# GpSimd's third block sum behind a lo part, and the short convolution's weight sums made by adding transfers

## The chip, the cores and the metric

One core of one Trainium2 chip runs the whole kernel. The metric is the time on the device in microseconds (us), the median over several runs. The core has TensorE (PE, matrix products), VectorE (DVE), ScalarE (ACT), GpSimd (POOL) and SyncE (SP), which run their own instruction lists in order and wait for each other by semaphores. Transfers between the chip's memory (DRAM) and the on-chip memory are issued from the queues of SP, ACT and POOL.

## The reference

One layer of a streaming encoder over 1024 positions and 1024 channels, all in float32:

```python
h = rms_norm(x, norm_mix_g[l]) * (1.0 + sc1) + sh1
proj = jnp.einsum('bsd,de->bse', h, w_in[l])
b_s, c_s, v_s, v_c, gl_c, gate_br = jnp.split(proj, SPLITS[:-1], axis=-1)
y_a = b_s * causal_dwconv(c_s * v_s, conv_short_w[l])
y_a = jnp.einsum('bsc,cd->bsd', y_a, w_short_out[l])
u = v_c * jax.nn.sigmoid(gl_c)
u = causal_dwconv(u, conv_conf_w[l]) + conv_conf_b[l]
u = jax.nn.silu(layer_norm(u, conf_ln_g[l], conf_ln_b[l]))
y_b = jnp.einsum('bsc,cd->bsd', u, w_conf_out[l])
g_a, g_b = jnp.split(jax.nn.sigmoid(gate_br), 2, axis=-1)
mix = jnp.einsum('bsd,de->bse', g_a * y_a + g_b * y_b, w_o[l])
x = x + g1 * mix
...
x = x + g2 * jnp.einsum('bsf,fd->bsd', jax.nn.silu(a) * bgate, w_ffn_out[l])
```

The change touches two of these products: `w_in` (the "input projection") and `w_short_out` (the "short convolution's projection", whose result is multiplied by the gate `g_a`).

## The kernel before

**Seven products instead of eight.** A weight is cut into "duals". A dual is two blocks of output rows by two halves of the inner dimension: four matrices of 128 x 1024 numbers, called 11, 12, 21 and 22. Its contribution is computed with seven products in the order 1, 2, 6, 5, 7, 3, 4 (`PRODUCTS`), in the manner of Strassen and Winograd. Products 1, 2 and 4 take the weights 11, 12 and 22 as they are. The others take sums: s1 = 21 + 22 (product 5), s2 = 11 + s1 (product 6), s3 = 21 + 11 (product 7), and 12 + s2 (product 3). These four block sums for each dual are the sums of the title.

**Hi and lo parts.** TensorE multiplies in a format with fewer bits, so every operand is split. ScalarE casts the weight to the hi part `wh` (line 234). VectorE or GpSimd subtracts: the lo part `wl` is the weight minus `wh` (line 235). Every product is 24 matmuls of 128 x 128 by 128 x 512: two output blocks, four inner blocks, and three combinations of hi and lo (lines 397, 398 and 400). Line 400 is the one that reads `wl`.

**Units.** The weight of one product, made ready, is a "unit": it loads what is missing into a `raw` buffer (line 218, on SP's queue), adds what has to be added, and calls `split_w`. `plan` lists the units, and `next_w` keeps two of them ready ahead of the product that runs. There are five raw buffers in this part of the kernel, and three each of `wh` and `wl`, so a unit's cast waits until the product three before it has left TensorE.

**The input projection** has 13 duals. `apart_units` makes the units of the first three, which the text calls the first, second and third input dual (d = 0, 1, 2). For the first, VectorE does sums and lo parts. For the second and third, GpSimd does the sums (line 312) and most lo parts: s1, s3 and s2 in product 6's unit, and 12 + s2 in product 3's. The third dual's products 1 and 2 run early, so that the products follow each other as: second dual 6, 5, 7, 3, 4, third dual 6, 5, ...

**The short convolution's projection** has two duals (0 and 1). Their 14 products run as 1, 1, 2, 2 (both duals), then 6, 5, 7, 3, 4 of dual 0 and the same of dual 1 (`ya_order`). `apart_units` makes these units too, with VectorE for all eight sums. Between the products VectorE also works on the other branch: it takes the mean from the convolution's result (`cv`, line 1015), adds up its squares (`sq`, line 1021), and splits the products' right sides (`q6l`, `q5l`, ..., line 913). `ya_evac` takes each product out of its accumulator and multiplies it by a gate tile `ga`, which is loaded from DRAM on GpSimd's queue (line 1088), 16 loads of 128 x 512.

**What sets the order.** The program is written once; a scheduler places the instructions of each engine and the transfers of each queue in a fixed list. `tc.issue_after(x)` tells it that an instruction has to stand behind x.

Of the kernel before, what the change touches and what calls it, by code (L numbers as in the profile page):

```python
# [38 lines left out]
ALU = mybir.AluOpType  # L39
# [76 lines left out]
PRODUCTS = "1265734"  # L116
# [15 lines left out]
def block_kernel(ctx: ExitStack, tc: tile.TileContext, x0, xT, c, vecs, ada, w_first, w_plain, w_duals,  # L132
                 w_short, w_conf, w_o, w_fi, w_fo0, w_fo1, outT):
    nc = tc.nc
# [30 lines left out]
    def ps2_tile(name):  # L165
        return ps2p.tile([P, H], F32, tag="ps2", name=name)
# [4 lines left out]
    def s_tile(name, dt=F32):  # L171
        return hl_tile(name, dt)

    def g_tile(name):
        return gsp.tile([P, H], F32, tag="gs", name=name)

    def f32(t):
        return t.bitcast(F32)

    halves = (slice(0, H), slice(H, T))  # L180
# [28 lines left out]
    def raw_tile(n=1024, home=None):  # L209

        if home is None:
            raws.append(raws.pop(0))
        return (home or raws[-1]).tile([P, 1024], F32, tag="raw", name="raw")[:, :n]

    def load(src, n=1024, home=None):
        raw = raw_tile(n, home)
        with tc.issue_after(x1_load[0]) if x1_load else ExitStack():
            load.ins = nc.sync.dma_start(raw, src).ins
        return raw
# [8 lines left out]
    def split_w(raw, n, after=(), lo_engine=nc.vector):  # L228
        wh = whp.tile([P, 1024], F32R, tag="wh", name="wh")[:, :n]
        wl = wlp.tile([P, 1024], F32R, tag="wl", name="wl")[:, :n]  # L230
        with ExitStack() as order:
            for ins in after:
                order.enter_context(tc.issue_after(ins))
            hi = nc.scalar.copy(wh, raw)  # L234
            lo = lo_engine.tensor_tensor(wl, raw, f32(wh), ALU.subtract)  # L235
        split_w.hi, split_w.lo = hi.ins, lo.ins
        if n == T and lo_engine is nc.gpsimd:
            pool_los.append((hi.ins, lo.ins))
        return wh, wl
# [66 lines left out]
    def apart_units(mats, eng, on_eng=PRODUCTS, after=None):  # L306


        a = {}

        def add(out, x, y):
            unit.eng.tensor_tensor(out, x, y, ALU.add)  # L312
            return out

        def get(b):
            return load(mats[("11", "12", "21", "22").index(b)])

        def unit(m):
            unit.eng = eng if m in on_eng else nc.gpsimd
            if m in "12":  # L320
                raw = get("1" + m)
            elif m == "6":
                for b in ("21", "22", "11"):
                    a[b] = get(b)
                with tc.issue_after(after()) if after else ExitStack():
                    a["s1"] = add(a["22"], a["21"], a["22"])
                    if "6" in on_eng:
                        raw = a["s2"] = add(raw_tile(), a["11"], a["s1"])
                    else:
                        a["s3"] = add(a["21"], a["21"], a["11"])  # L330
                        raw = a["s2"] = add(a["11"], a["11"], a["s1"])
            elif m == "7":
                raw = a["s3"] if "s3" in a else add(a["21"], a["21"], a["11"])
            elif m == "3":
                raw = get("12")
                add(raw, raw, a["s2"])
            else:
                raw = a["s1"] if m == "5" else get("22")
            return split_w(raw, 1024, (), unit.eng)

        return {m: (lambda m=m: unit(m)) for m in PRODUCTS}

    plan = [None] * KC
    plan += [(w_plain[0], 1024)]
    n_duals = len(PAIRS) // 2
    win_units = [apart_units([w_duals[d, m] for m in range(4)], nc.vector, PRODUCTS if d == 0 else "125" if d == 1 else "12",
                             (lambda: t_split.ins) if d == 1 else None) for d in range(BEGUN + 1)]
    win_units += [dual_units([w_duals[d, m] for m in range(4)], 1024, eng=nc.gpsimd) for d in range(BEGUN + 1, n_duals)]
    win_order = [(BEGUN, m) for m in "12"] + [(d, m) for d in range(BEGUN + 1) for m in PRODUCTS[2:]]
    win_order += [(d, m) for d in range(BEGUN + 1, n_duals) for m in PRODUCTS]  # L350
    plan += [win_units[d][m] for d, m in win_order]
    ya_order = [(d, m) for m in "12" for d in range(2)] + [(d, m) for d in range(2) for m in PRODUCTS[2:]]
    ya_units = [apart_units([w_short[d, m] for m in range(4)], nc.vector) for d in range(2)]
    plan += [ya_units[d][m] for d, m in ya_order]
    plan += [(w[k], 1024) for w in (w_conf, w_o) for ks in (range(KC), SECOND[KEPT:]) for k in ks]
    ready = []
# [212 lines left out]
    gate_dram = {(b, j): dram.tile([P, T], F32, name=f"gate_{b}{j}") for b in "ab" for j in range(KC)}  # L569
# [173 lines left out]
    def plus(out, ps, b):  # L743
        plus.ins = nc.vector.tensor_tensor(out, ps, b, ALU.add).ins
# [150 lines left out]
    b = {}  # L895
# [185 lines left out]
    def ya_evac(d, banks):  # L1081

        st = {}

        def out(i, row, h, op, ps):
            j = 4 * d + 2 * i + row
            ga = g_tile("ga")
            nc.gpsimd.dma_start(ga, gate_dram["a", j][:, halves[h]])
            ma[j, h] = s_tile(f"ma{j}{h}")
            op(ma[j, h], ps, ga)  # L1090
            ma["ins"] = plus.ins

        def evac(i, m, ps):
            if m == "1":
                if d == 1:
                    banks["y", i] = ps2_tile("y")
                nc.scalar.copy(banks["y", i], ps)
            elif m in "65":
                st[m, i] = s_tile("vz")
                nc.scalar.copy(st[m, i], ps)  # L1100
            elif m == "2":
                out(i, 0, 0, times, ps)
            elif m == "7":
                z = ps2_tile("z")
                plus(z, ps, st["5", i])
                out(i, 1, 1, minus_times, z)
            elif m == "3":
                plus(ps, ps, st["6", i])
                out(i, 0, 1, times, ps)
            else:  # L1110
                out(i, 1, 0, minus_times, ps)
        return evac
# [577 lines left out]
```

## Time and profile before

| what | value |
|---|---|
| median of 3 runs | 1460.13 us (1459.64, 1460.13, 1461.17) |
| the profiled execution, its time | 1462.66 us |
| its span, first to last instruction | 1460.9 us |
| TensorE's granted clock | 0.999 |
| busy: TensorE, VectorE, ScalarE, GpSimd | 1448.1, 1188.5, 627.2, 516.3 us |
| the input projection's stage, roughly | 90 to 562 us |
| the short convolution's projection | 562.2 to 643.0 us |

The durations in the prediction are from this one execution. Its time is 1.8 us above its span (what lies around the first and last instruction) and 2.5 us above the median of the runs without a profile, so a saving found in the trace is taken off the median. A timeline row reads: start, duration, engine, line, operation, output<-inputs, shapes and count; in brackets how long the engine was idle just before and what ended that idle time. "PEld" is TensorE's weight load, "SPq" and "POOLq" the transfer queues of these engines.

### The profile page before, as it was taken

The page shows a single profiled execution, that of the slowest core. Times are in us where ns is not written, and L with a number is a line of the kernel's source. Part 1 is how long each engine was busy: PE and PEld are TensorE (multiplying, and loading weights), DVE is VectorE, ACT ScalarE, POOL GpSimd, SP SyncE. Part 2 cuts the span into 40 slices and gives each one's busy share as a digit, 9 for nine tenths or more (in the row PEclk, how much of TensorE's full clock was granted, in tenths as well). Part 3 has the DMA queues.
Part 4 walks back from the last instruction along what each step waited for, and adds up shares of the span by engine and source line. Part 5 has one row for each costly group of instructions (what it writes and reads, how often), then busy time and mean ns, then how long its engine had stood idle before and what let it go on. Part 6 is the DMA issues. An engine that isn't in the chain of part 4 may idle for free.

```text
span 1460.9 us, 17711 instructions
## 1 busy us (share of the span) xinstructions
PE 1448.1 (99%) x6394; PEld 1187.8 (81%) x6394; DVE 1188.5 (81%) x1634; ACT 627.2 (43%) x911; POOL 516.3 (35%) x484
## 2 busy tenths in 40 slices
PE   9999999999999999999999999999999999999997
PEld 4878888888888888788888888888888888888887
DVE  7897999987988979999787698777777666866676
ACT  4773333333333346465235465444444443322235
POOL 0007777677677761111021001111111005662505
PEclk9999999999999999999999999999999999999999
DMA  9542222323222357476685436655554449996903
GB/s 351 206 139 85 73 94 79 116 73 101 72 87 73 123 201 281 130 233 206 209 293 203 152 101 216 214 178 198 169 177 148 143 148 327 395 392 193 359 1 116
DMA packets 88522, 257.68 MB, mean 176 GB/s; under 512 B 10177, under 2 KB 12865, under 8 KB 88434
## 3 DMA queue, kind: packets, MB, share of 16 engines
q1 hardware_dynamic: 43792, 142.04, 29.1%
q0 software_dynamic: 40608, 101.92, 21.2%
q10 hardware_dynamic: 4034, 12.59, 2.4%
q8 instruction: 50, 0.82, 0.2%
q14 instruction: 38, 0.31, 0.1%
HBM read 190.97 MB, written 65.54 MB: 176 GB/s over the span
## 4 chain that ended last, share of the span: by engine, by line
PE 88%; issue 4%; DVE 3%; POOL 2%; DMA 1%; ACT 1%; POOLq 0%; DVEq 0%; ACTq 0%
PE bank L400 11%; PE bank L397 11%; PE bank L398 11%; PE x L400 8%; PE x L398 8%; PE x L397 8%; PE z L397 3%; PE z L398 3%; PE z L400 3%; PE mix L400 2%; PE mix L397 2%; PE yb L400 2%; PE yb L397 2%; PE mix L398 2%; PE yb L398 2%
## 5 line engine op out<-in xcount | busy, mean ns | idle before, releaser
L234 ACT CAST wh<-raw 128x1024 fp32r<-128x1024 f32 (+3 forms) x255 | 260.9, 1026 | 475.5 <-PE bank L398 149.5
L235 DVE TENSOR_TENSOR wl<-raw,wh 128x1024 fp32r<-128x1024 f32 (+3 forms) x176 | 209.1, 1190 | 49.3 <-ACT wh L234 46.6
L235 POOL TENSOR_TENSOR wl<-raw,wh 128x1024 fp32r<-128x1024 f32 x79 | 191.4, 2426 | 105.4 <-ACT wh L234 105.3
L972 DVE SCALAR_TENSOR_TENSOR c<-diff,vec,c 128x512 f32<-128x512 f32 x232 | 168.4, 752 | 2.7
L1331 POOL DMA_DIRECT2D hid<-stage x70 | 37.3, 533 | 343.9 <-DVE stage L438 332.5
L400 PE MATMUL bank<-th,wl 128*128 128x512 f32 x312 | 121.5, 389 | 0.4 <-POOL wl L235 0.4
L398 PE MATMUL bank<-tl,wh 128*128 128x512 f32 x312 | 121.4, 389 | 0.0
L397 PE MATMUL bank<-th,wh 128*128 128x512 f32 x312 | 121.4, 389 | 0.0
L972 DVE SCALAR_TENSOR_TENSOR c<-u,wsum,c 128x512 f32<-128x512 f32 x112 | 84.4, 753 | 2.3
L400 PEld LDWEIGHTS bank<-th,wl 128*128 128x128 f32 x312 | 58.6, 188 | 13.0 <-POOL wl L235 0.8
L398 PEld LDWEIGHTS bank<-tl,wh 128*128 128x128 f32 x312 | 58.6, 188 | 12.2
L398 PE MATMUL x<-tl,wh 128*128 128x512 f32 x176 | 68.5, 389 | 0.0
L397 PE MATMUL x<-th,wh 128*128 128x512 f32 x176 | 68.5, 389 | 0.0
L400 PE MATMUL x<-th,wl 128*128 128x512 f32 x176 | 68.4, 390 | 0.0
L397 PEld LDWEIGHTS bank<-th,wh 128*128 128x128 f32 x312 | 58.6, 188 | 12.1
L437 ACT CAST stage<-g 128x512 fp32r<-128x512 f32 x60 | 37.3, 621 | 68.0 <-DMA hid<-stage 42.9
L438 DVE TENSOR_TENSOR stage<-g,stage 128x512 fp32r<-128x512 f32 x60 | 41.3, 690 | 27.2 <-ACT stage L437 27.1
L1355 POOL DMA_DIRECT2D th<-hid x77 | 41.2, 535 | 53.5 <-PE x L400 23.4
L312 POOL TENSOR_TENSOR raw<-raw 128x1024 f32<-128x1024 f32 x8 | 20.5, 2567 | 110.0 <-ACT th L437 104.9
L400 PE MATMUL yb<-zsh,wl 128*128 128x512 f32 x128 | 49.8, 389 | 0.0
L397 PE MATMUL yb<-zsh,wh 128*128 128x512 f32 x128 | 49.8, 389 | 0.0
L398 PE MATMUL yb<-zsl,wh 128*128 128x512 f32 x128 | 49.8, 389 | 0.0
(829 smaller groups left out, 4135.4 us busy)
## 6 DMA issues: line engine op xcount, KB each, us to landing
hid<-stage POOLq DMA_DIRECT2D x70, 512.0 KB, 4.7
raw<-in_w_duals SPq DMA_DIRECT2D x57, 512.0 KB, 3.5
raw<-in_w_fi SPq DMA_DIRECT2D x54, 512.0 KB, 4.7
th<-hid POOLq DMA_DIRECT2D x77, 256.0 KB, 6.0
tl<-hid POOLq DMA_DIRECT2D x77, 256.0 KB, 6.1
ada<-in_ada SPq DMA_DIRECT2D x24, 512.0 KB, 5.7
raw<-in_ada SPq DMA_DIRECT2D x24, 512.0 KB, 4.9
raw<-in_w_fo SPq DMA_DIRECT2D x16, 512.0 KB, 6.1
```

Source lines behind the costliest of these rows:

```text
L234: hi = nc.scalar.copy(wh, raw)
L235: lo = lo_engine.tensor_tensor(wl, raw, f32(wh), ALU.subtract)
L312: unit.eng.tensor_tensor(out, x, y, ALU.add)
L397: nc.tensor.matmul(ps, wh, xh, start=first, stop=False, skip_group_check=again)
L398: nc.tensor.matmul(ps, wh, xl, start=False, stop=False, skip_group_check=again)
L400: mm3.ins = nc.tensor.matmul(ps, wl, xh, start=False, stop=last, skip_group_check=again).ins
L437: t_split.act = nc.scalar.copy(hi, src).ins
L438: t_split.ins = nc.vector.tensor_tensor(lo, src, f32(hi), ALU.subtract).ins
L972: tap.ins = nc.vector.scalar_tensor_tensor(out=out, in0=src[:, s : s + H], scalar=wt, in1=acc, op0=ALU.mult, op1=ALU.add).ins
L1331: nc.gpsimd.dma_start(hid_dram[key], s)
L1355: nc.gpsimd.dma_start(t, hid_dram[key][:, s])
```

## The change

It has three parts.

1. In `apart_units`, where s2 is not on VectorE, GpSimd's s2 is ordered behind the lo part that was made last. For the third input dual this is GpSimd's own lo part of the second dual's product 4.
2. The short convolution's units come from a new function, `added_units`. Three of the four sums of each dual are made by a transfer that adds to what lies in the raw buffer (`accum_op`), issued on GpSimd's queue: 21 onto 22 (s1), 11 onto a fresh 21 (s3), and 12 onto s2. VectorE keeps one sum for each dual, s2. Loads on SP for each dual go from seven to six, and there are three adding transfers beside them. The raw buffers that a dual uses go from six to four (and products 1 and 2's).
3. The 16 gate loads `ga` move from GpSimd's queue to SP's.

```diff
                     else:
                         a["s3"] = add(a["21"], a["21"], a["11"])
-                        raw = a["s2"] = add(a["11"], a["11"], a["s1"])
+                        with tc.issue_after(split_w.lo):
+                            raw = a["s2"] = add(a["11"], a["11"], a["s1"])
...
+    def added_units(mats):
+
+
+        a = {}
+        mat = dict(zip(("11", "12", "21", "22"), mats))
+
+        def add(raw, b):
+            nc.gpsimd.dma_start(raw, mat[b], accum_op=ALU.add)
+            return raw
+
+        def unit(m):
+            if m == "6":
+                a["s1"] = add(load(mat["22"]), "21")
+                raw = a["s2"] = load(mat["11"])
+                nc.vector.tensor_tensor(raw, raw, a["s1"], ALU.add)
+            elif m == "7":
+                raw = add(load(mat["21"]), "11")
+            elif m == "3":
+                raw = add(a["s2"], "12")
+            else:
+                raw = a["s1"] if m == "5" else load(mat[{"1": "11", "2": "12", "4": "22"}[m]])
+            return split_w(raw, 1024)
...
-    ya_units = [apart_units([w_short[d, m] for m in range(4)], nc.vector) for d in range(2)]
+    ya_units = [added_units([w_short[d, m] for m in range(4)]) for d in range(2)]
...
             ga = g_tile("ga")
-            nc.gpsimd.dma_start(ga, gate_dram["a", j][:, halves[h]])
+            nc.sync.dma_start(ga, gate_dram["a", j][:, halves[h]])
```

In the changed kernel the lines behind the new function have numbers higher by 26; the sum on VectorE is its line 358, the adding transfer its line 351, the gate load its line 1114.

**First place: GpSimd, where the third input dual's sums are made.** Before:

```order
L235 TENSOR_TENSOR wl<-raw,wh 128x1024
L312 TENSOR_TENSOR raw<-raw 128x1024 x2
L235 TENSOR_TENSOR wl<-raw,wh 128x1024
L312 TENSOR_TENSOR raw<-raw 128x1024 x2
L235 TENSOR_TENSOR wl<-raw,wh 128x1024 x6
L254 TENSOR_TENSOR raw<-raw 128x1024
```

Now:

```order
L235 TENSOR_TENSOR wl<-raw,wh 128x1024
L312 TENSOR_TENSOR raw<-raw 128x1024 x2
L235 TENSOR_TENSOR wl<-raw,wh 128x1024 x2
L312 TENSOR_TENSOR raw<-raw 128x1024 x2
L235 TENSOR_TENSOR wl<-raw,wh 128x1024 x5
L254 TENSOR_TENSOR raw<-raw 128x1024
```

The first pair of L312 is the third dual's s1 and s3, the second pair its s2 and 12 + s2. The lo part of the second dual's product 4 stood behind the second pair and stands ahead of it now. Nothing else on this engine moves until the short convolution.

**Second place: VectorE, in the short convolution's projection, where dual 1's product 6 is made ready** (`z`, `bank` are accumulators, `vz` what was copied out of one, `ma` the gated results). Before:

```order
L751 TENSOR_SCALAR ma_4819<-z,ga 128x512
L1015 TENSOR_TENSOR cv_4821<-cv_4821,mu_4514 128x512
L1015 TENSOR_TENSOR cv_4821<-cv_4821,mu_4518 128x512
L312 TENSOR_TENSOR raw<-raw 128x1024
L1021 TENSOR_TENSOR sq<-sq 128x512 x2
L312 TENSOR_TENSOR raw<-raw 128x1024
L744 TENSOR_TENSOR bank<-bank,vz 128x512 x2
L235 TENSOR_TENSOR wl<-raw,wh 128x1024
L747 TENSOR_TENSOR ma_4859<-bank,ga 128x512
```

Now:

```order
L777 TENSOR_SCALAR ma_4816<-z,ga 128x512
L1041 TENSOR_TENSOR cv_4818<-cv_4818,mu_4514 128x512
L1041 TENSOR_TENSOR cv_4818<-cv_4818,mu_4518 128x512
L358 TENSOR_TENSOR raw<-raw 128x1024
L1047 TENSOR_TENSOR sq<-sq 128x512 x2
L235 TENSOR_TENSOR wl<-raw,wh 128x1024
L770 TENSOR_TENSOR bank<-bank,vz 128x512 x2
L773 TENSOR_TENSOR ma_4853<-bank,ga 128x512
```

The s1 of dual 1 is gone, s2 stands in its place, and the lo part of product 6 (L235) stands two instructions nearer to it.

**Third place: SP's queue, from the last loads of `cv` on.** Before:

```order
L1013 DMA cv_4924<-cv_931 128x1024
L218 DMA raw<-in_w_short 128x1024 x6
L218 DMA raw<-in_w_conf 128x1024 x2
L218 DMA raw<-in_w_short 128x1024
L218 DMA raw<-in_ada 128x1024
```

Now:

```order
L1039 DMA cv_4918<-cv_931 128x1024
L218 DMA raw<-in_w_short 128x1024 x2
L1114 DMA ga<-gate_a_108 128x512
L1114 DMA ga<-gate_a_110 128x512
L218 DMA raw<-in_w_short 128x1024
L1114 DMA ga<-gate_a_112 128x512
L1114 DMA ga<-gate_a_114 128x512
L218 DMA raw<-in_w_short 128x1024 x2
L1114 DMA ga<-gate_a_109 128x512
L1114 DMA ga<-gate_a_111 128x512
L218 DMA raw<-in_w_conf 128x1024
```

The gate loads stand between the weight loads now. On GpSimd's queue the 16 gate loads are replaced by six rows `L351 DMA raw<-in_w_short 128x1024`, the adding transfers. TensorE's list is the same in both kernels. Behind the projection the five raw buffers are taken up at another point of their turn, so that some later loads and VectorE rows, up to the feed-forward part, stand in a slightly different order.

More of the change, by code (lines that the diff above doesn't have):

```diff
@@ L339, in unit @@
             return split_w(raw, 1024, (), unit.eng)
+        return {m: (lambda m=m: unit(m)) for m in PRODUCTS}
+    def added_units(mats):
[16 more added lines that the diff above has]
+            return split_w(raw, 1024)
         return {m: (lambda m=m: unit(m)) for m in PRODUCTS}
```

## The prediction

> **What bounds the kernel now.** I read the first lines of the page, the chain that ended last by engine, and what TensorE waited for.
>
> ```profile
> span 1460.9 us, 17711 instructions
> PE 1448.1 (99%) x6394; PEld 1187.8 (81%) x6394; DVE 1188.5 (81%) x1634; ACT 627.2 (43%) x911; POOL 516.3 (35%) x484
> PE 88%; issue 4%; DVE 3%; POOL 2%; DMA 1%; ACT 1%; POOLq 0%; DVEq 0%; ACTq 0%
> PE bank L400 <- DVE wl L235: 0.5, 1, 0.5
> PE bank L400 <- POOL wl L235: 0.4, 1, 0.4
> PE z L397 <- DVE g L1296: 0.2, 1, 0.2
> ```
>
> TensorE works for 1448.1 of 1460.9 us, and the change takes no matmul away. So it can only win what TensorE waits for, and these waits are few. The view of waits (who waited, for whom, total, times, longest, in us) has one on a lo part of VectorE, one on a lo part of GpSimd and one in the feed-forward part. The question is therefore which of these the change touches, and whether it makes a new one. All numbers are from the one profiled execution, with its span of 1460.9 us and its time of 1462.66 us; the median without a profile is 1460.13 us, and I take savings off that.
>
> Next, TensorE's own timeline at the first two of these waits:
>
> ```profile
> 148.01 0.39 PE L397 MATMUL bank<-th,wh 128*128 128x512 f32 x1
> 148.24 0.39 PE L398 MATMUL bank<-tl,wh 128*128 128x512 f32 x1
> 149.05 0.50 PE L400 MATMUL bank<-th,wl 128*128 128x512 f32 x1 [0.42 <-POOL wl L235]
> 149.38 0.39 PE L397 MATMUL bank<-th,wh 128*128 128x512 f32 x1
> ...
> 612.68 0.39 PE L400 MATMUL bank<-q4h,wl 128*128 128x512 f32 x1
> 613.09 0.50 PE L397 MATMUL bank<-q6h,wh 128*128 128x512 f32 x1
> 613.43 0.39 PE L398 MATMUL bank<-q6l,wh 128*128 128x512 f32 x1
> 614.35 0.50 PE L400 MATMUL bank<-q6h,wl 128*128 128x512 f32 x1 [0.53 <-DVE wl L235]
> 614.69 0.40 PE L397 MATMUL bank<-q6h,wh 128*128 128x512 f32 x1
> ```
>
> Undisturbed matmuls start 0.23 us apart (148.01 to 148.24). The idle time in brackets understates a stall, since matmuls overlap; the starts tell it. At 148 the gap is 0.81 us and the next 0.33 us, so the stall costs 0.58 + 0.10 = **0.7 us**. This is product 4 of the second input dual. At 613 the four gaps are 0.41, 0.34, 0.92 and 0.34 us, which makes 0.18 + 0.11 + 0.69 + 0.11 = **1.1 us**. This is dual 1's product 6 in the short convolution's projection. Together 1.8 us, 0.12% of the span. That is all the change aims at.
>
> **The first part: GpSimd's third sum.** GpSimd and ScalarE around the stall:
>
> ```profile
> 137.10 1.05 ACT L234 CAST wh<-raw 128x1024 fp32r<-128x1024 f32 x1 [1.91 <-PE bank L398]
> 142.97 1.05 ACT L234 CAST wh<-raw 128x1024 fp32r<-128x1024 f32 x1 [4.33 <-POOL raw L312]
> ...
> 138.18 2.40 POOL L235 TENSOR_TENSOR wl<-raw,wh 128x1024 fp32r<-128x1024 f32 x1
> 140.54 2.40 POOL L312 TENSOR_TENSOR raw<-raw 128x1024 f32<-128x1024 f32 x1
> 144.24 2.40 POOL L312 TENSOR_TENSOR raw<-raw 128x1024 f32<-128x1024 f32 x1 [1.30 <-DMA raw<-in_w_duals]
> 146.59 7.12 POOL L235 TENSOR_TENSOR wl<-raw,wh 128x1024 fp32r<-128x1024 f32 x3
> ```
>
> The first of the three lo parts at 146.59 is the one TensorE waits for: it ends at 149.0. Its cast was over at 138.15. Ahead of it stood s2 (140.54), then 1.3 us of waiting for a load, then 12 + s2 (144.24). With the new order it runs from 140.54 to 142.9, over 5 us before TensorE takes it at 148.5. The stall goes.
>
> What is late next? s2 moves from 140.54 to 142.9 and ends at 145.3. Its cast, which follows s2 (the row at 142.97), runs from 145.3 to 146.4. On GpSimd 12 + s2 follows from 145.3 to 147.7 (its load is there since 144.24), and the lo part of the third dual's product 6 from 147.7 to 150.1. TensorE wants that lo part three matmuls into the next product, which starts at 148.01 + 24 x 0.227 = 153.5 us when nothing stalls. The cover is 3.4 + 0.5 us, and without it each us late would cost one. The following lo part was the third of the merged row (to 153.7) and ends at 152.5 now. Nothing else on GpSimd or its queue is passed. So −0.7 us, with bounds of −0.7 and 0.
>
> **The second part: fewer sums on VectorE.** How full VectorE is in this stage (stretch, its length, then busy us and count for TensorE, its weight loads, VectorE, ScalarE, GpSimd; clock, DMA share, GB/s), and its rows that matter:
>
> ```profile
> 585.70:612.70 27.00, 27.00 (x121) 22.34 (x119) 26.78 (x39) 12.79 (x20) 3.22 (x6) 1.00 0.43 137
> ...
> 567.73 1.23 DVE L312 TENSOR_TENSOR raw<-raw 128x1024 f32<-128x1024 f32 x1
> 570.17 1.22 DVE L312 TENSOR_TENSOR raw<-raw 128x1024 f32<-128x1024 f32 x1 [0.62 <-DMA raw<-in_w_short]
> 572.52 1.22 DVE L235 TENSOR_TENSOR wl<-raw,wh 128x1024 fp32r<-128x1024 f32 x1
> 577.73 1.22 DVE L235 TENSOR_TENSOR wl<-raw,wh 128x1024 fp32r<-128x1024 f32 x1
> 593.55 1.31 DVE L747 TENSOR_TENSOR ma<-y,ga 128x512 f32<-128x512 f32 x2 [0.22 <-DMA ga<-gate_a]
> 597.71 1.22 DVE L312 TENSOR_TENSOR raw<-raw 128x1024 f32<-128x1024 f32 x1
> 598.84 1.29 DVE L1021 TENSOR_TENSOR sq<-sq 128x512 f32<-128x512 f32 x2
> 608.33 1.23 DVE L312 TENSOR_TENSOR raw<-raw 128x1024 f32<-128x1024 f32 x1
> 610.67 1.23 DVE L312 TENSOR_TENSOR raw<-raw 128x1024 f32<-128x1024 f32 x1
> 613.07 1.23 DVE L235 TENSOR_TENSOR wl<-raw,wh 128x1024 fp32r<-128x1024 f32 x1
> ```
>
> VectorE is busy 26.78 of the 27 us ahead of the stall. Its backlog is what makes TensorE wait: s2 of dual 1 comes only at 610.67, its lo part at 613.07. A sum takes 1.13 us of its time (597.71 to 598.84). Up to that s2, the change removes the sums s3 of dual 0 (570.17, with 0.62 us of waiting), 12 + s2 (597.71) and s1 of dual 1 (608.33), and s2 of dual 0 takes the place of s1 (567.73), one more gone. The two after 593 lead to 2.3 us earlier even if a wait for `ga` at 593.5 swallows the two before it; all four would give 4.5 + 0.6 us. The lo part also passes two 0.6 us instructions in the new order. TensorE needs the lo part at 613.36 (three matmuls of 0.227 behind 612.68) and got it at 614.35, so 1.0 us is needed, and 2.3 at least is there. The stall goes: −1.1 us, bounds −1.1 and 0 (no gain, if something else holds VectorE).
>
> The price is six adding transfers, which the trace does not have. Nearest rows (KB each, median us from issue to landing), and where the first would stand:
>
> ```profile
> raw<-in_w_short SPq DMA_DIRECT2D x14, 512.0 KB, 3.9
> cv<-cv SPq DMA_DIRECT2D x8, 512.0 KB, 7.0
> x<-x_dram POOLq DMA_DIRECT2D x8, 512.0 KB, 5.6
> ga<-gate_a POOLq DMA_DIRECT2D x16, 256.0 KB, 4.1
> ...
> 549.59 0.33 SPq L218 DMA_DIRECT2D raw<-in_w_short  x1
> 558.90 5.67 SPq L218 DMA_DIRECT2D raw<-in_w_short  x2
> 549.53 3.44 POOL L993 TENSOR_TENSOR tot<-tot,u 128x512 f32<-128x512 f32 x2
> 575.28 0.39 PE L400 MATMUL bank<-q2h,wl 128*128 128x512 f32 x1
> ```
>
> An adding transfer of 512 KB should take no less than a plain load, 3.9 us. From above I bound it by reading the target and writing it back as two more passes at the slowest row: 3 x 7.0 = 21 us, an estimate. I take twice GpSimd's plain 512 KB load, 11 us, since that is the same queue and size, and adding has a second operand to read.
>
> The first adding transfer (21 onto 22 of dual 0) can go when the load issued at 549.59 has landed (553.5 with 3.9 us) and GpSimd is past its two additions (553.0). With 11 us it lands at 564.5. VectorE wants it at 567.73, where s2 of dual 0 stands now; its other operand, loaded at 558.90, is there by 563. So it is hidden with 3 us to spare. If it came later, VectorE would stand with the q5 and q6 splits and product 2's lo part behind it. That lo part would end at 571.9 now (572.52 + 1.13, less the removed 1.13 and 0.62), and TensorE needs it at 575.28. So TensorE waits only once the transfer takes **over 17.6 us** (564.5 + 3.2 + 3.4 against 11), and from there one us for each.
>
> The next ones have about as much room. A product takes 24 x 0.227 = 5.44 us, so behind product 2 of dual 0, which starts at 574.8, its products 6, 7 and 3 start at 585.7, 596.6 and 602.0, and dual 1's product 3, three behind the 613 of its product 6, at about 629. 11 onto a fresh 21 has its load issued by 564.6 (the end of the pair at 558.90), and is wanted some 2.5 us of cast and lo part ahead of 596.6. 12 onto s2 goes once product 6's lo part is made (577.73 before, ended at 578.9) and is wanted at 599.5: 20 us. For dual 1 the tightest is 12 onto s2: behind a lo part that ends at about 611, for 629 less 2.5 us, 16 us, and a few short sums of TensorE's in between give one more. All of it is a queue's work; GpSimd has nothing else to do here (3.22 of 27 us). Cost: 0, with the estimate of 21 us as the upper bound: 3 to 5 us.
>
> By the Trainium skill (Collectives: The Full Stack, "The bandwidth ceiling: the fold count and why AG ≠ RS ≠ AR") the adding itself is free, but an adding transfer reads two sources and so runs at about half the rate of a copy. Twice the row of 5.6 us is what I took; the skill's rule would leave the sum as it is and eats two thirds of the margin, and no run here shows it yet.
>
> **The third part: the gate loads on SP's queue.** Sixteen issues of 0.33 us (the row at 549.59) are nothing on a queue that mostly waits. What counts is order: a gate load stands behind weight loads that wait for lo parts, and the other way round. The second pair stood at 588.8 for VectorE at 593.5. It stands behind one load that waits for product 5's lo part, some 2 us earlier than before, and so comes no later. The weight loads behind gate loads are for products at least 20 us on. Cost 0; a pair that came late by 3 us would still only use up part of VectorE's gain.
>
> **Sum.** −0.7 − 1.1 + 0 = −1.8 us: 1460.13 − 1.8 = **1458.3 us**. Its own range is 1457.6 (the waits behind go as well) to 1459.3.
>
> **Rivals.** *One of the two gains fails:* the wait only moves. Against it stand 3.9 us of cover on GpSimd and over 1 us on VectorE; for it, that VectorE stays nearly full and now also waits for transfers. Price: 0.7 to 1.1 of the 1.8 us, so 1459.0 to 1459.6, up to 1460.2 if both fail.
>
> *The adding transfers are late:* slower. Place: VectorE at 567.7, in order, and TensorE at 575.3. It decides from 17.6 us for 512 KB; slower than before from about 19.4 us, by over 0.2% from 22.4 us. At 25 us: −1.8 + 7.4, 1465.7 us. For it: adding may read, add and write in the transfer engines, which no row shows. Against it: 17.6 us is three times the GpSimd row of the same size. The skill's halved rate above leaves it unlikely too.
>
> *A new wait behind the projection:* the raw buffers are taken up at another point of their turn, and VectorE's list changes in the feed-forward part, where one wait stands (`z` on line 1296 above). VectorE and loads have slack nearly everywhere there, but every product is a place where one can come. I price a few at 0.7 to 1.1 us, the size of the two above, so up to +5 − 1.8: 1460 to 1463.5. It may as well take the present wait away (−0.6).
>
> **How the numbers follow.** Forecast (both stalls go) 0.55; one or both gains fail 0.12; late adding transfers 0.18; new waits behind 0.11; more gained than the sum 0.04. The late transfers have more than the rows alone would give them, since the change puts an operation into the kernel whose time no row shows. A measurement of this kernel tells about 0.2%, 2.9 us, from no change, so "faster" is below 1457.2 and "slower" above 1463.1. Faster is the last case, 0.04: all waits of TensorE that I can name in reach add up to less than 2.9 us. Slower is most of the late transfers (0.15) and half of the new waits (0.06): 0.21. Within 0.2%: 0.75. The range that holds 8 in 10 goes from 1457.2 to 1464.0: it takes in the failed gains, the upper bound of 21 us and the new waits, and leaves out transfers beyond 23 us.
>
> **What would show it.** GpSimd's lo part ends near 143 and TensorE shows no gap near 148; the product after it starts near 153.5 rather than 154.2. In the projection, TensorE has no gap at dual 1's product 6, and VectorE has idle time where 26.78 of 27 us were busy. The adding transfers land in 8 to 14 us, and no row of VectorE or ScalarE waits for them. The prediction is wrong if adding transfers take over 20 us, if VectorE stands at line 358, or if TensorE has a new wait on a lo part or a cast.

## The result

| | median us | lowest to highest | executions |
|---|---|---|---|
| before | 1461.27 | 1459.64 to 1462.97 | 10 |
| changed | 1464.52 | 1463.09 to 1466.00 | 10 |

The ratio is 1.0021, with a 95% interval from 1.0013 to 1.0030: the change costs about 3.1 us. The forecast was 1458.3 us, faster, with a range up to 1464.0 us. The kernel is slower, and 0.5 us beyond the range. The forecast took its gains off a median of three runs, 1460.13 us; over ten runs the kernel before takes 1461.27 us. Counted from there the range would have held the 1464.52 us, but not the sign.

### The profile page after: what moved, and what is told of

The parts are those of the page before. It is cut to its first block, busy times and chain, and to the rows that moved or that the text cites. A ratio compares the mean times of both kernels' runs of the same rounds, so it can differ in the third digit from the quotient of the medians.

```text
span 1463.3 us, 17722 instructions
## 1 busy us (share of the span) xinstructions
PE 1449.2 (99%) x6394; PEld 1189.8 (81%) x6394; DVE 1181.8 (81%) x1628; ACT 628.2 (43%) x911; POOL 512.9 (35%) x474
## 4 chain that ended last, share of the span: by engine, by line
PE 93%; DVE 2%; DMA 2%; issue 1%; POOL 1%; ACT 0%; POOLq 0%; DVEq 0%; ACTq 0%; SPq 0%
PE bank L426 12%; PE bank L423 12%; PE bank L424 12%; PE x L426 8%; PE x L423 8%; PE x L424 8%; PE z L423 4%; PE z L426 4%; PE z L424 4%; PE yb L426 2%; PE yb L424 2%; PE mix L424 2%; PE mix L423 2%; PE mix L426 2%; PE yb L423 2%; PE y L426 2%
## 5 line engine op out<-in xcount | busy, mean ns | idle before, releaser
L235 DVE TENSOR_TENSOR wl<-raw,wh 128x1024 fp32r<-128x1024 f32 (+3 forms) x176 | 209.0, 1189 | 65.6 <-ACT wh L234 61.9
L235 POOL TENSOR_TENSOR wl<-raw,wh 128x1024 fp32r<-128x1024 f32 x79 | 191.6, 2427 | 105.6 <-ACT wh L234 105.5
L312 POOL TENSOR_TENSOR raw<-raw 128x1024 f32<-128x1024 f32 x8 | 20.3, 2539 | 108.2 <-DMA raw<-in_w_duals 104.1
```

## Where the time went: the profile after

First the head of the changed kernel's page, and what TensorE waited for in it (total, times, longest, in us).

```profile
span 1463.3 us, 17722 instructions
PE 1449.2 (99%) x6394; PEld 1189.8 (81%) x6394; DVE 1181.8 (81%) x1628; ACT 628.2 (43%) x911; POOL 512.9 (35%) x474
PE z L423 <- DVE g L1322: 3.2, 1, 3.2
PE bank L426 <- DVE wl L235: 0.3, 1, 0.3
```

The wait on GpSimd's lo part and the long one on VectorE's lo part are gone, as forecast (the 0.3 us left stands at another place, near 595 us). One wait has grown: `z` on VectorE's line 1322 is 3.2 us long. It is the wait on line 1296 of the kernel before, where it was 0.2 us. It lies in the feed-forward part, some 270 us behind the last line that the change touches.

The loss and the gains can be laid out along TensorE's list, which is the same in both kernels. The starts of the same matmul in the two timelines:

| matmul | before us | after us | after less before | step |
|---|---|---|---|---|
| last `lead<-h31h,wl` | 73.98 | 72.98 | −1.00 | −1.00, ahead of everything changed |
| first `mu<-tot,ones` | 567.62 | 565.83 | −1.79 | −0.79 |
| first `var<-sq,ones` | 624.95 | 622.59 | −2.36 | −0.57 |
| first `z<-t5h,wh` of the late product | 911.54 | 909.18 | −2.36 | 0 |
| first `x<-t7h,wh` behind it | 917.53 | 919.76 | +2.23 | **+4.59** |
| last `z` row ahead of the tail | 1430.83 | 1433.09 | +2.26 | 0 |

The first step is not the change's: in the profiles of this study that matmul starts anywhere from 72.77 to 74.14 us. Without it the two traces say −0.79 − 0.57 + 4.59 = +3.2 us, as much as the medians are apart. That the sums agree so well is in part luck: the −0.57 holds a stall of 1.1 us at 613 us that other executions of the kernel before don't have (below).

**The one product that lost 4.6 us.** TensorE's timeline of the changed kernel there:

```profile
911.67 0.39 PE L426 MATMUL z<-t5h,wl 128*128 128x512 f32 x1
915.30 0.50 PE L423 MATMUL z<-t5h,wh 128*128 128x512 f32 x1 [3.24 <-DVE g L1322]
915.64 0.55 PE L424 MATMUL z<-t5l,wh 128*128 128x512 f32 x1
915.99 0.63 PE L426 MATMUL z<-t5h,wl 128*128 128x512 f32 x1
916.42 0.63 PE L423 MATMUL z<-t5h,wh 128*128 128x512 f32 x1
...
918.55 0.63 PE L426 MATMUL z<-t5h,wl 128*128 128x512 f32 x1
918.98 0.47 PE L423 MATMUL z<-t5h,wh 128*128 128x512 f32 x1
919.29 0.40 PE L424 MATMUL z<-t5l,wh 128*128 128x512 f32 x1
```

Two losses stand in these rows. From 911.67 to 915.30 is 3.63 us where 0.23 is due: **3.4 us** of waiting. Then the matmuls start 0.34 and 0.35 us apart, and from 915.99 to 918.98 us 0.43 us apart, instead of 0.23. The product takes 919.76 − 909.18 = 10.58 us instead of 5.44, so 5.14 us are lost, and 5.14 − 3.40 = **1.7 us** of it comes after TensorE is at work again. The windows show why. Each row has the stretch, its length, busy us and count of TensorE, its weight loads, VectorE, ScalarE and GpSimd, then the granted clock, the share of the transfer engines (in short stretches the view can give more than 1), and GB/s; first the changed kernel:

```profile
905.00:920.00 15.00, 11.76 (x46) 9.20 (x45) 10.82 (x16) 6.61 (x12) 3.72 (x7) 0.89 0.91 290
915.80:918.00 2.20, 2.20 (x7) 1.71 (x6) 2.20 (x3) 1.56 (x4) 0.00 (x0) 0.50 0.99 279
```

and the kernel before, the same stretches:

```profile
905.00:920.00 15.00, 14.78 (x65) 11.90 (x64) 13.61 (x19) 9.66 (x15) 3.72 (x7) 1.00 0.65 210
915.80:918.00 2.20, 2.20 (x12) 1.78 (x11) 1.65 (x2) 1.72 (x4) 0.26 (x1) 1.00 1.14 371
```

The granted clock is 0.50 behind the wait (7 matmuls in 2.2 us instead of 12). And the transfer engines are 91% busy around the wait, where they were 65% before.

**Followed back from the wait.** VectorE in the changed kernel; line 1322 empties an accumulator (`y`) that TensorE needs:

```profile
909.67 0.69 DVE L464 TENSOR_TENSOR stage<-t,stage 128x512 fp32r<-128x512 f32 x1
911.71 0.69 DVE L464 TENSOR_TENSOR stage<-g,stage 128x512 fp32r<-128x512 f32 x1 [1.34 <-ACT stage L463]
913.96 0.69 DVE L464 TENSOR_TENSOR stage<-g,stage 128x512 fp32r<-128x512 f32 x1 [1.55 <-ACT stage L463]
914.56 0.68 DVE L1322 TENSOR_TENSOR g<-y,g 128x512 f32<-128x512 f32 x1
```

and ScalarE, for which it waits:

```profile
908.64 0.62 ACT L463 CAST stage<-t 128x512 fp32r<-128x512 f32 x1 [2.61 <-issue]
911.05 0.62 ACT L463 CAST stage<-g 128x512 fp32r<-128x512 f32 x1 [1.79 <-DMA hid<-stage]
913.30 0.62 ACT L463 CAST stage<-g 128x512 fp32r<-128x512 f32 x1 [1.63 <-DMA hid<-stage]
```

The kernel before has the same VectorE instructions in the same order, without a wait:

```profile
911.93 0.69 DVE L438 TENSOR_TENSOR stage<-t,stage 128x512 fp32r<-128x512 f32 x1
912.53 1.44 DVE L438 TENSOR_TENSOR stage<-g,stage 128x512 fp32r<-128x512 f32 x2
913.89 0.69 DVE L1296 TENSOR_TENSOR g<-y,g 128x512 f32<-128x512 f32 x1
```

`stage` has three buffers. Each is filled by a cast and a subtraction and stored to DRAM (`hid`) from GpSimd's queue; a cast waits until the store three before it has landed. So late stores make ScalarE late, then VectorE, whose list is in order, then the emptying of `y`, then TensorE. Why the stores are late is seen in the transfers issued from 903 to 912 us (count, KB each, median us from issue to landing) and in SP's queue; the changed kernel:

```profile
hid<-stage POOLq DMA_DIRECT2D x3, 512.0 KB, 5.4
...
903.84 0.33 SPq L218 DMA_DIRECT2D raw<-in_w_fi  x1
906.18 0.33 SPq L218 DMA_DIRECT2D raw<-in_w_fi  x1
```

and the kernel before, where SP has no load between 887.74 and the row below:

```profile
hid<-stage POOLq DMA_DIRECT2D x2, 512.0 KB, 3.1
...
915.78 1.61 SPq L218 DMA_DIRECT2D raw<-in_w_fi  x2
```

Two weight loads leave at 903.84 and 906.18 us that left at 915.78 us or later before, and the stores beside them take 5.4 us instead of 3.1. The loads are 22 and 21 of the feed-forward dual 3. They leave as soon as their raw buffer is free. Which buffer that is hangs on the list `raws`, from which the raw buffers are taken in turn: three of one pool, two of another, and from the feed-forward part on a sixth, which is appended to the list where it stands at that moment. The new units take two buffers less for each dual, four less in all, so with five in the turn the list stands one place further at the append. Before, no load left between 887.74 us and the end of the lo part of the previous dual's product 7 (915.7 us); now the two get buffers that are free as soon as the lo parts of its products 6 and 5 are made (903.8 and 906.2 us).

## The experiments

They ask first whether the order of the buffers alone does it, then whether it is the traffic of the two loads, then what the rest of the change is worth. All ratios are to the kernel before, timed on the same chip beside them: 1461.04 us (29 executions) for the list turned back, the list turned on in the kernel before, the first part alone and the first run with the gate loads back, and 1460.90 us (33 executions) for the other four.

**The list turned back.** In the changed kernel:

```diff
             rawap = open_pool("raw_a", 1, side="right", stack=ctx)[1]
+            raws.insert(0, raws.pop())
             raws.append(rawap)
```

> The changed kernel, with the list of raw buffers turned back by one place at the point where the sixth buffer joins it (feed-forward part), so that the buffers follow each other there in the order they had before the change. Theory A (the loss comes from the order of the buffers alone: in the changed kernel two weight loads are issued at 903.84 and 906.18 us instead of 915.78 and 916.88, beside the stores of hid, and TensorE waits 3.4 us at 911.67 and then runs 13 matmuls at a lower clock): the two loads stand behind the 7's lo part again, the gap at 911 is at most 0.6 us, the granted clock of that stretch is 1.00, and the time is 4.6 us under the changed kernel's: 1459.9 us beside 1461.3 before, ratio 0.999. Rival B (the stall comes from what stands ahead: TensorE arrives 1.4 to 2.4 us earlier and VectorE, or the ScalarE casts, cannot follow): the gap stays over 3 us, 1464.5 us, ratio 1.002.

Measured: 1461.15 us, ratio 0.9999 (0.9990 to 1.0008). TensorE's row at the place, and the stores issued from 903 to 912 us:

```profile
913.00 0.50 PE L423 MATMUL z<-t5h,wh 128*128 128x512 f32 x1
...
hid<-stage POOLq DMA_DIRECT2D x4, 512.0 KB, 3.3
```

The matmul before it started at 912.67, so TensorE's longest gap there is 0.34 us between starts, and the stores land in 3.3 us. The loss is gone, so Rival B is out: TensorE reaches this matmul 838.7 us after the first row of the table above in both kernels (912.67 − 73.95 here, 911.67 − 72.98 in the changed one), and now it doesn't wait. The time is not the 1459.9 us expected, though the interval holds it; more on that below.

**The list turned on, in the kernel before:**

```diff
             rawap = open_pool("raw_a", 1, side="right", stack=ctx)[1]
+            raws.append(raws.pop(0))
             raws.append(rawap)
```

> The kernel before, with only the list of raw buffers turned on by one place where the sixth buffer joins it: the feed-forward part takes the buffers in the changed kernel's order, nothing else differs. Theory A: two loads are issued some 12 us earlier, the gap of over 3 us and the lower clock appear near 914 us, and the time is 4.6 us above before: 1465.9 us, ratio 1.003. Rival B: the order of the buffers is harmless by itself, 1461.3 us, ratio 1.000, gap 0.6 us as before.

Measured: 1464.83 us, ratio 1.0027 (1.0017 to 1.0038). One line that computes nothing makes the kernel before as slow as the changed one. What TensorE waited for, its timeline, and the hid stores issued from 903 to 912 us:

```profile
PE z L397 <- DVE g L1296: 2.6, 1, 2.6
...
915.25 0.80 PE L397 MATMUL z<-t5h,wh 128*128 128x512 f32 x1 [2.60 <-DVE g L1296]
...
hid<-stage POOLq DMA_DIRECT2D x3, 512.0 KB, 5.8
```

The wait is at the same place, behind stores of 5.8 us. The loss is 3.8 us where 4.6 was expected; the wait is 2.60 us here and 3.24 in the changed kernel.

**Only the two loads held back.** The changed kernel, its buffers in its own order; `hold` is set for dual 3 alone:

```diff
             elif m == "1":
-                get("11", "12", "21", "22")
+                get("11", "12")
+                with tc.issue_after(load.ins) if hold else ExitStack():
+                    get("21", "22")
```

> The changed kernel; in the feed-forward dual 3 the loads of 21 and 22 stand behind the load of 12 on SP's queue. The buffers are taken in the changed kernel's order, everything else is as in it. Theory A, second step (it is the traffic of these two loads that makes the stores of hid land late): issued behind the load of 12 they leave at 914 us or later, the stores issued near 905 and 907 us land in 3 to 3.5 us instead of 5.5 to 5.9, ScalarE's cast does not wait, the gap at 911 is at most 0.7 us, and the time is that of the ring turned back: 1461 us, ratio 1.000. Rival C (the order of the buffers does its harm in another way, by the order of VectorE's list or by which instruction frees which buffer): the gap stays, 1464.5 us, ratio 1.0025.

Measured: 1460.33 us, ratio 0.9998 (0.9989 to 1.0007). TensorE's row at the place, and the stores issued from 903 to 912 us:

```profile
912.93 0.50 PE L425 MATMUL z<-t5h,wh 128*128 128x512 f32 x1 [0.72 <-DVE g L1324]
...
hid<-stage POOLq DMA_DIRECT2D x4, 512.0 KB, 3.3
```

The loads leave from 915.17 us on, the stores land in 3.3 us again, and the wait shrinks to 0.72 us (1.11 us between starts, where at most 0.7 was expected). So it is the time at which these two loads leave that costs; Rival C is out. That the loads and the stores share the transfer engines is what the 91% and 65% above suggest; no run took away the traffic and left the issue times.

**Two more places of the list.** The changed kernel with the list turned on by one and by three more places (`for _ in range(1)` or `range(3)`: `raws.append(raws.pop(0))`).

> The changed kernel with the list of raw buffers turned on by one more place where the sixth buffer joins it (the two buffers of one pool come first behind the new one). Theory A says that any order has its own times at which loads can leave, so that the gap depends on where two loads meet the stores of hid: a time other than the two seen so far is possible, between 1459 and 1466 us; if the order did nothing by itself it would be 1464.5 us as the changed kernel.

> The changed kernel with the list of raw buffers turned on by three more places (all three buffers of the first pool behind the new one, then the two of the other). Theory A: a time of its own between 1459 and 1466 us, with the gap near 911 following the issue times of the two loads of dual 3; if they leave before 910 us a gap over 1.5 us, if later, none. If the order did nothing by itself, 1464.5 us.

Measured: 1460.72 us, ratio 0.9999 (0.9990 to 1.0008), and 1463.47 us, ratio 1.0017 (1.0008 to 1.0026). In the first the loads leave at 914.39 us, and TensorE's wait is 0.66 us; in the second at 903.07 and 905.41 us, with a wait of 2.43 us. Both follow the rule that was written down for the second: leave before 910 us, and lose. (The fifth possible turn of the list was not run.)

**The first part alone.** The kernel before with GpSimd's s2 behind the lo part:

> The kernel before with only the first part of the change (GpSimd's s2 of the third input dual behind the lo part of the second dual's product 4). If the working of the first part is right: the 0.81 us gap near 148 us is gone, no other gap appears, 0.7 us under before: 1460.6 us, ratio 0.9995. Rival (the wait only moves to the third dual's products): a new gap between 150 and 165 us and no gain, ratio 1.000.

Measured: 1459.97 us, ratio 0.9993 (0.9984 to 1.0002). Its trace has no gap near 148 us and none behind it, and none of its waits of TensorE is on GpSimd. The 0.7 us expected lies in the interval, but so does nothing. It also has no gap near 613 us, though the second part of the change isn't in it.

**The gate loads back on GpSimd's queue**, the rest of the change kept:

```diff
-            nc.sync.dma_start(ga, gate_dram["a", j][:, halves[h]])
+            nc.gpsimd.dma_start(ga, gate_dram["a", j][:, halves[h]])
```

> The changed kernel with the gate loads back on GpSimd's queue, nothing else undone. Theory: in the changed kernel VectorE stands 2.58 us at 592.6 for a gate load that was issued at 585.24 behind a weight load that waited until 584.31, and TensorE's new gap at 595 (0.44 + 0.11 us) follows from it. With the gate loads on their old queue that wait and the gap go: 0.55 us under the changed kernel, 1464.0 us; the gap at 911 stays, since the buffers are taken in the same order: ratio 1.0018. Rival 1: the gate loads stand behind the adding transfers on GpSimd's queue and come later still: a gap at 595 as long or longer, 1464.5 to 1466. Rival 2: the gap at 911 is gone as well, 1459.5, so that it came from the gate loads and not from the order of the buffers.

Measured: a median of 1464.31 us over ten executions, ratio 1.0025 (1.0014 to 1.0035), and wider than any other: 1461.01 to 1468.94 us. (An eleventh took 3801.66 us; nothing here explains it, and it is left out of these figures.) The profiled one was the shortest; it has no gap at 595 and one of 1.87 us between starts at 911. With the list of buffers turned back as well:

> The changed kernel with the list of raw buffers turned back by one place and the gate loads back on GpSimd's queue: both costs undone, the first part and the adding transfers kept. If the two costs are all there is: no gap at 148, 595, 613 or 911, 0.6 us under the kernel with the ring alone turned back and 0.7 to 1.3 us under before: 1460.0 us, ratio 0.9993. Rival (the gate loads on GpSimd's queue stand behind adding transfers in some executions and come late): 1461 us or more, with a wide spread.

Measured: 1461.88 us, ratio 1.0011 (1.0001 to 1.0020), from 1459.42 to 1465.33 us. Its profiled execution, the shortest again at 1459.42 us, has none of the four gaps, yet the median lies 0.7 us over that of the list turned back alone. The rival, with its wide spread, is what came. The traces of these two kernels were taken again, to see a long execution.

> The kernel of e6_back_ga once more, for its trace alone: its executions spread from 1459.4 to 1465.3 us, and the profiled one was a short one. Theory D: in the long executions a gate load on GpSimd's queue stands behind an adding transfer that waits, VectorE waits for it between 570 and 650 us, and TensorE has a gap of 2 to 4 us there with a lower clock behind it. Rival E: the gap is at 911 us again, since the two loads, though later, sometimes still meet the stores of hid. An execution under 1461 us shows neither and leaves it open.

> As e9_back_ga_look, a second trace of the same kernel, since about half of its executions were long. Theory D: a long one has its gap between 570 and 650 us; rival E: at 911 us.

> The kernel of e4_ga_pool once more, for its trace alone (1461.0 to 1468.9 us there, the profiled one the shortest). Theory D: an execution over 1464 us has gaps in two places, one between 570 and 650 us of 2 us or more, and the one at 911. Rival E: one place only, 911, with a gap of 3 us or more. The gap at 911 alone is worth up to 5 us (1.4 + 3.6), so 1468 us cannot be reached by rival E.

The first took 1460.46 us and has no gap worth naming. The second took 1461.76 us and shows the place; VectorE and TensorE in it:

```profile
588.19 0.69 DVE L773 TENSOR_TENSOR ma<-bank,ga 128x512 f32<-128x512 f32 x1 [3.54 <-DMA ga<-gate_a]
589.69 0.69 DVE L773 TENSOR_TENSOR ma<-bank,ga 128x512 f32<-128x512 f32 x1 [0.81 <-DMA ga<-gate_a]
...
595.39 0.39 PE L424 MATMUL bank<-q7l,wh 128*128 128x512 f32 x1
597.58 0.50 PE L426 MATMUL bank<-q7h,wl 128*128 128x512 f32 x1 [1.80 <-DVE wl L235]
```

A gate load that stands behind an adding transfer on GpSimd's queue comes late (the transfer was issued at 581.97 us, after 5.12 us of waiting for a load, and the gate loads from 582.50 on; in the kernel before they were issued at 578.13 and 579.86), VectorE waits 3.54 + 0.81 us for it, and TensorE loses about 2.1 us six us later: theory D. The third trace (1464.26 us) has a small gap at 595 and 3.07 us at 911, nearer to rival E. No execution over 1465 us was caught, so the longest ones stay open.

## Why the prediction was wrong

**The first part: right.** In the changed kernel GpSimd makes the two lo parts in one go, and its sums follow:

```profile
137.30 4.76 POOL L235 TENSOR_TENSOR wl<-raw,wh 128x1024 fp32r<-128x1024 f32 x2
142.02 4.91 POOL L312 TENSOR_TENSOR raw<-raw 128x1024 f32<-128x1024 f32 x2
```

The needed lo part is over at 142.0 us, the gap is gone, and nothing behind it waits. The term was −0.7; the timelines show −0.79 between 74 and 567 us.

**The second part: the stall is gone, but the term was too large.** The window of the changed kernel that answers to the 27 us shown before:

```profile
585.00:612.00 27.00, 26.72 (x118) 21.77 (x118) 24.42 (x37) 12.96 (x20) 1.72 (x2) 1.00 0.70 178
```

VectorE is busy 24.42 us where it was 26.78, the lo part of dual 1's product 6 is in time, and there is no gap near 613. But in the traces of the list turned on and of the first part alone, whose code is that of the kernel before there, there is no gap near 613 us either. So the 1.1 us is no fixed cost of that code; it stood in the one execution that was profiled, whose 1462.66 us lay 1.4 us above the median of its kernel. Nor does it come from VectorE's fullness, as the prediction read it. In the trace of the list turned on, VectorE is just as full, but it enters the stage earlier:

```profile
585.70:612.70 27.00, 27.00 (x121) 22.36 (x120) 26.79 (x39) 13.58 (x21) 3.22 (x6) 1.00 0.42 137
...
564.71 1.21 DVE L312 TENSOR_TENSOR raw<-raw 128x1024 f32<-128x1024 f32 x1
```

That is the first sum of the stage. It starts 2.3 us ahead of TensorE's first `mu<-tot` there (567.02 us), and in the profiled execution of the kernel before 0.1 us behind it (567.73 and 567.62). Of the thirteen traces of this study five are late in this way: before, changed, the list turned back, the loads held, and the list turned on by one. (In the other eight the sum starts 0.4 to 3.0 us ahead.) The last four of the five have the second part in them, and none of them has a gap near 613 us. This speaks for a stall that comes in late executions only and that the second part takes away; a single trace has the stall, so how often it comes stays open.

The medians agree: the kernels without the loss (the list turned back, the loads held) come out at 0.9999 and 0.9998, and not 1.8 us under before, which would be 0.9988 and lies just outside both intervals (from 0.9990 and 0.9989). A gain of up to some 1.5 us is neither shown nor excluded.

**The adding transfers: right.** Their row for the stretch of 554 to 620 us, beside plain loads and gate loads of the same time:

```profile
raw<-in_w_short SPq DMA_DIRECT2D x7, 512.0 KB, 5.6
raw<-in_w_short POOLq DMA_DIRECT2D x6, 512.0 KB, 8.1
ga<-gate_a SPq DMA_DIRECT2D x10, 256.0 KB, 6.1
```

They land in 5.5 to 8.7 us, under the assumed 11 (and partly under the 8 to 14 that were named as a sign) and far under the 17.6 from which it would cost, and no instruction is listed as waiting for them. The Trainium skill (Collectives: The Full Stack, "The bandwidth ceiling: the fold count and why AG ≠ RS ≠ AR") has the reduce step of a ring at about half the rate of a copy step, since it reads two sources. What is measured here is 8.1 to 5.6 us, a factor of 1.4, between two queues.

**The third part: "Cost 0" was wrong by half a us in the profiled execution.** SP's queue and VectorE in the changed kernel, and the gap that follows:

```profile
584.31 0.33 SPq L218 DMA_DIRECT2D raw<-in_w_short  x1
585.24 1.01 SPq L1114 DMA_DIRECT2D ga<-gate_a  x2
592.60 1.30 DVE L773 TENSOR_TENSOR ma<-y,ga 128x512 f32<-128x512 f32 x2 [2.58 <-DMA ga<-gate_a]
595.69 0.50 PE L426 MATMUL bank<-q7h,wl 128*128 128x512 f32 x1 [0.28 <-DVE wl L235]
```

The pair was to be issued some 2 us earlier than before (588.8); it was, by 3.6 us (1.8 of them because TensorE reaches this stage earlier in this execution, 565.83 for 567.62 us), and still came late: it took 7.4 us (585.24 to 592.60), where it had taken 4.7 (588.8 to 593.5), and VectorE was there 2.58 us sooner. TensorE loses about 0.5 us by it (0.67 us between starts where 0.23 is due, and 0.34 for the next), and it isn't in every execution (the trace with the loads held has no gap there, that of the list turned back has). Yet the move itself was needed: with the gate loads left on GpSimd's queue behind adding transfers, executions spread over 6 to 8 us.

**The step that failed** is what the sum puts behind the projection: nothing. The feed-forward part stands only in the rival "A new wait behind the projection". It named the mechanism (the raw buffers "are taken up at another point of their turn") and even the wait, `z` on line 1296. It then priced a new wait at 0.7 to 1.1 us, "the size of the two above" (a few of them up to +5 in all), and gave the case 0.11 for a reason that doesn't hold at this place: "VectorE and loads have slack nearly everywhere there". The kernel before waited there already: its accumulator `y` came free 0.2 us too late. There was no slack, so the 1.34 + 1.55 us that VectorE waited behind the late stores went through to TensorE. One wait of 3.24 us instead of 0.22 came of it, and 1.7 us of low clock on top, which no case of the prediction had. The second error of the sum is the −1.1: it was taken as a fixed cost of the kernel before, and two other traces of that code don't have it. The order of the loads in the feed-forward part was known ahead; its difference was taken as slight, and it was not followed to the stores.

## What to carry to other kernels

A change in the number of buffers that a stage takes from a shared turn can move the loads of later stages, here some 270 us behind it: look where the kernel already waits behind the change, and price what stands there with no slack at the full lateness of its transfers, plus the clock. Where loads can run ahead of stores that are awaited, fix their order by a dependency, as the held loads do, rather than by where the turn happens to stand. And a stall of 1 us in one profiled execution is a term of the sum only if other executions of the same code have it.

## What the runs showed of the hardware

**In these traces the clock fell behind waits of 2.43 us and more, and not behind waits of 1.80 us and less.** TensorE's idle time and what followed; the 1.80 us is the wait at 597.58 us shown above, the others are those near 911 us:

| trace | TensorE idle us | 0.43 us between matmuls behind it |
|---|---|---|
| loads held | 0.72 | no |
| gate loads on GpSimd (e4) | 1.47 | no |
| gate loads on GpSimd, list back (e11) | 1.80 | no |
| list turned on by three more | 2.43 | from 915.35 |
| list turned on, kernel before | 2.60 | from 915.84 |
| gate loads on GpSimd (e10) | 2.68 | from 916.08 |
| changed kernel | 3.24 | from 915.99 |

In the fourth of these TensorE first ran 1.5 us (913.84 to 915.35) at or near its full rate:

```profile
913.84 0.51 PE L423 MATMUL z<-t5h,wh 128*128 128x512 f32 x1 [2.43 <-DVE g L1322]
914.18 0.40 PE L424 MATMUL z<-t5l,wh 128*128 128x512 f32 x1
...
915.12 0.41 PE L426 MATMUL z<-t5h,wl 128*128 128x512 f32 x1
915.35 0.62 PE L423 MATMUL z<-t5h,wh 128*128 128x512 f32 x1
915.76 0.63 PE L424 MATMUL z<-t5l,wh 128*128 128x512 f32 x1
...
918.75 0.40 PE L426 MATMUL x<-t7h,wl 128*128 128x512 f32 x1
```

The slow stretch lasts 918.75 − 915.35 = 3.4 us and costs some 1.6 us (half of its matmuls' places). The Trainium skill (TensorE: Matmul & The Clock Gate, "Part 1: The HAM clock gate") describes a half-rate clock after an idle window of about 3.4 us that runs freely. The half rate (426.7 ns for 512 columns there, 0.43 us here) agrees. A slow stretch of 3.4 us stands in this trace; in the other three the rows that are 0.43 us apart cover 2.1 to 3.0 us. The idle time ahead of it was as short as 2.43 us here.

**Stores took longer beside loads of the same size.** At the same place the 512 KB stores of `hid` took 3.1 to 3.3 us (median) in the kernel before, with the loads held and with the list turned by one, and 5.2 to 5.8 us beside two 512 KB loads in the changed kernel and in the lists turned on. The first of these loads landed in 3.5 us itself in the changed kernel (the landing of the second is not in the trace), which is no more than the 4.3 us (median) of all these loads in the changed kernel: the stores took longer, and this load did not.
